# A head's inverse norm brought to all partitions: four transposes on TensorE, or two transfers through DRAM

## The chip, the core and the metric

The kernel runs on one core of a Trainium2 chip. The metric is device time in microseconds (us) of one execution; several executions are run and their median is taken.

The core's engines are called by the profile's names: PE is TensorE (matrix products, and transposes as products with an identity matrix; PEld is its weight load), DVE is VectorE, ACT is ScalarE, POOL is GpSimd, SP is SyncE, which here only issues DMA transfers. POOL issues some transfers too. Each engine works through its own list of instructions in order; when an instruction waits, everything behind it on that engine waits too.

## What is computed

The reference is an encoder trunk of two layers on 512 tokens. The change touches one spot of it, the norm at the end of differential attention. Cut to that:

```python
def diff_attention(qa, ka, va, ..., subln_g, lam_init, cos, sin):
    ...
        s = jnp.einsum('bhcqd,bhckd->bhcqk', qi, k).astype(f32) * scale
        a = jax.nn.softmax(s, axis=-1)
        a = (a[:, :, 0] - lam * a[:, :, 1]).astype(v.dtype)
        return jnp.einsum('bhqk,bhkd->bhqd', a, v)
    ...
    o = rmsnorm(o, subln_g) * (1.0 - lam_init)

def rmsnorm(x, g):
    y = x32 * lax.rsqrt(jnp.mean(x32 * x32, axis=-1, keepdims=True) + EPS)
    return (y * g.astype(jnp.float32)).astype(x.dtype)
```

There are 4 heads and 2 layers, so this norm is computed 8 times. Each time the output `o` of a head has 512 tokens of 128 values; every token has one inverse norm, by which its 128 values are multiplied. The result `ya` goes through `w_br_a`, together with the outputs of a convolution branch and of a neighbourhood attention branch, each under a sigmoid gate. After that come an output projection, a feed-forward block and an embedding gate.

## The kernel before, in words

Activations lie transposed: the 128 partitions hold channels, the free dimension holds the 512 tokens. Nearly all products are made in three parts: a number is split into a high and a low half (`split`, line 162: ACT copies the high half, DVE subtracts to get the low half), and `mm3` (line 175) adds high by high, high by low and low by high. Weights come from DRAM over SP's queue into tile `wr`, are split into `wh` and `wl` by ACT and DVE (`weights`, line 166), and are used by PE; each of these tiles has three buffers. `weights` also keeps the DVE instruction of its low half as `self.low`, and plans the whole load and split some way ahead of its place in the program.

**The order of the work.** PE's instructions run in exactly the order in which the program writes them. For the other engines a planner orders the instructions at build time by priority, which follows the place in the program, and by modelled durations; the chip then runs each engine's list in that fixed order. `behind(i, then)` (line 1064) adds an edge to the planner: instruction `i` comes after `then` on their engine. It adds no wait on the chip.

The program interleaves small jobs with the long projections by a clock of its own. `chunk` (line 115) counts one `mm3` of a 512-column projection; every fourth calls `tick` (line 94). A job is a generator: it emits some instructions, yields a number of ticks, and is continued after so many. `later` (line 107) queues a job with a delay and a gap to the next.

**The layer.** `layer` (line 428) writes: the convolution's gates, neighbourhood attention (four `natten_in`), differential attention (four `diff_in`, one for each head, with other projections between them), the gates for the third branch (`gate_c`), the third branch itself (`branch_c`: eight outputs, one tick each, added into `acc`, tile `gatec_x`), gates of the second branch (`gate_b`), `merge_a` (the first branch's gate and its product with `w_br_a`; the heads' results `ys` are read here), the rest of the convolution, `merge_b`, `w_o`, the feed-forward block and the embedding gate. The 124 taps of the convolution are single DVE instructions (`taps`, line 535), strewn as `background` work over the whole first part of the layer.

**A head.** `diff_in` (line 813) makes queries and keys and queues four `diff_unit` jobs, two ticks apart. Each computes scores for 128 queries (`probs`, line 892: PE scores into one of the two PSUM buffers `sc`, DVE maximum, ACT exponential, DVE combination `diff_a`). Every second job goes on (line 851): after three ticks PE transposes the probabilities, ACT and DVE split them into tile `pt`; after two more ticks PE multiplies with the values into `av`. After the fourth job the head is complete: ACT squares `av` into `sq` (tile tag `ss`, one buffer only) and writes the scaled output `o` (tag `t`). Then `norm` (line 206) runs with the ticks `(1, 2)`:

- after one tick, PE transposes `sq` in four pieces into a PSUM tile (line 213), DVE sums over channels (line 216) and adds the epsilon term (line 221), and POOL raises to the power -0.5 (line 223). The result `col` is a column: partition p, column c holds the inverse norm of token 128c + p.
- after two more ticks, PE transposes each of the four columns of `col`, spread over 128 columns, into a second PSUM tile `bc` (line 227). Every partition then holds the row of all 512 inverse norms.
- `done` (line 884): DVE multiplies `o` by that row (line 885; the profile lists it at line 157, where the helper stands, as diff_t), and ACT and DVE split the product into a tile `y` (five buffers, four of which hold the neighbourhood attention's output until `branch_c` has read it).

The same `norm` serves the main norms and the convolution's norm; these copy the row from PSUM to SBUF (`spread`) and are not changed.

Of the kernel before, what the change touches and what calls it, by code (L numbers as in the profile page):

```python
# [11 lines left out]
F32 = mybir.dt.float32  # L12
# [3 lines left out]
ALU = mybir.AluOpType  # L16
# [4 lines left out]
P = 128  # L21
L = 2
S = 512
# [4 lines left out]
HA = 4  # L28
# [33 lines left out]
class Net:  # L62
# [143 lines left out]
    def norm(self, sq, n, waits, done, spread=True, eps=None):  # L206


        nc = self.nc
        yield waits[0]  # L210
        st = self.ps("tr", (P, 4, P))
        for c in range(4):
            nc.tensor.transpose(st[:, c, :], sq[:, c * P:(c + 1) * P], self.ident)
        with self.tc.high_priority(offset=min(200, self.tc.cur_priority - self.p0) if n == D and self.p0 is not None else 0):
            sm = self.sb("sm", [P, 4])
            nc.vector.tensor_reduce(out=sm, in_=st, op=ALU.add, axis=AX.X)
            ms = self.sb("sm", [P, 4])
            if eps is None:
                nc.vector.tensor_scalar(ms, sm, 1.0 / n, EPS, ALU.mult, ALU.add)
            else:  # L220
                self.stt(ms, sm, 1.0 / n, eps, ALU.mult, ALU.add)
            col = self.sb("rc", [P, 4])
            nc.gpsimd.tensor_tensor(col, ms, self.power, ALU.pow)
        yield waits[1]
        bc = self.ps("tr", (P, 4, P))
        for c in range(4):
            nc.tensor.transpose(bc[:, c, :], col[:, c:c + 1].to_broadcast([P, P]), self.ident)
        bc = bc.rearrange("p a b -> p (a b)")
        done(col, self.spread(bc) if spread else bc)

    def rows(self, col, rb):
        self.col, self.rb = col, rb
# [59 lines left out]
    def build(self):  # L292
        nc, tc, a = self.nc, self.tc, self.a
        self.bufs = dict(wr=3, wh=3, wl=3, h=8, qk=2, kh=2, v=4, pt=2, y=5, z=5, x=4, t=7, rp=4,
                         e=4, a=3, r=2, rb=1, ss=1, sm=8, rc=4, b=2, s=8)
        self.bg, self.w_ahead = BG, 400
        self.pbufs = dict(mm=3, sc=2, tr=2, av=1)
        with tc.tile_pool(name="sb", bufs=1) as self.pool, \
                tc.tile_pool(name="ps", bufs=1, space=PSUM) as self.psum, \
                tc.tile_pool(name="dr", bufs=1, space=DRAM) as dram:  # L300
            xs = dram.tile([KD, P, 512], F32, name="xs")
            self.pis = dram.tile([KD, P, 512], F32, name="pis")
            with tc.manual_schedule(engines={mybir.EngineType.PE}):
                h = self.opening()
                xsrc = a["xT"]
                for i in range(L):
                    h = self.layer(i, h, xsrc, xs)
                    xsrc = xs
# [535 lines left out]
    def diff_unit(self, head, qt, st4, k2, st, box, ys):  # L844

        nc, i = self.nc, self.i
        half, t = qt // 2, qt % 2
        box[qt] = self.probs(st4, k2, qt, box["s0"])
        if t == 0:
            return  # L850
        yield 3
        ats = [box[2 * half], box[2 * half + 1]]
        pps = []
        for kp in range(2):
            pt = self.ps("tr", (P, 2, 256))
            for u in range(2):
                for t in range(2):
                    kc = 2 * kp + u
                    nc.tensor.transpose(pt[:, u, t * P:(t + 1) * P],
                                        ats[t][:, kc * P:(kc + 1) * P], self.ident)  # L860
            pp = self.sb("pt", [P, 2, 2, 256], F32R)
            self.split(pp[:, 0], pp[:, 1], pt)
            pps.append(pp)
        yield 2
        if half == 0:
            box["av"] = self.ps("av")
        av = box["av"]
        cs = slice((head % 2) * P, (head % 2) * P + P)
        for kp in range(2):
            for u in range(2):  # L870
                v = st["v", head // 2][kp][:, u].rearrange("p (a b) -> p a b", a=2)
                self.mm3(av[:, half * 256:half * 256 + 256], v[:, 0, cs], v[:, 1, cs],
                         pps[kp][:, 0, u], pps[kp][:, 1, u], kp * 2 + u == 0, kp * 2 + u == 3)
        if half == 0:
            return

        eps = self.sb("sm", [P, 4])
        self.stt(eps, box["s0"], EPS, box["s0"], ALU.mult, ALU.mult)
        o = self.sb("t", [P, 512])
        sq = self.sb("ss", [P, 512])  # L880
        self.act(sq, av, AF.Square)
        self.act(o, av, AF.Copy, scale=self.subg[:, i:i + 1])

        def done(col, bc):
            self.tt(o, o, bc, ALU.mult)
            y = self.sb("y", [P, 2, 512], F32R)
            self.split(y[:, 0, :], y[:, 1, :], o)
            ys.append(y)

        yield from self.norm(sq, P, (1, 2), done, spread=False, eps=eps)  # L890

    def probs(self, st4, k2, qt, s0):


        nc, i = self.nc, self.i
        qs = slice(qt * P, (qt + 1) * P)
        m = self.sb("s", [P, 10])
        es = []
        for u in range(2):
            sc = self.ps("sc")  # L900
            self.scores(sc, st4, k2, u, qs, slice(0, 512))
            nc.vector.tensor_reduce(out=m[:, u:u + 1], in_=sc, op=ALU.max, axis=AX.X, negate=True)  # L902
            e = self.sb("e" if u else "a", [P, 512])
            self.act(e, sc, AF.Exp, table="exp", bias=m[:, u:u + 1],
                     accum_out=m[:, 3:4] if u else s0[:, qt:qt + 1])
            es.append(e)
        nc.vector.reciprocal(m[:, 4:5], m[:, 3:4])
        self.stt(m[:, 5:6], m[:, 4:5], self.nlam[:, i:i + 1], s0[:, qt:qt + 1],
                 ALU.mult, ALU.mult)
        self.stt(es[0], es[1], m[:, 5:6], es[0], ALU.mult, ALU.add)  # L910
        return es[0]

    def w_o(self, mg, xsrc):
# [553 lines left out]
```

## Time and profile before

| | |
|---|---|
| median of 3 runs | 1777.44 us (1776.35 to 1777.76) |
| span of the profiled execution, first to last instruction | 1776.7 us |
| PE busy in it | 1767.5 us, 99% |
| DVE, ACT, POOL busy | 80%, 50%, 6% |
| granted TensorE clock | 0.999 of full speed |

Of the profiled execution the span is all that is listed; the median of the runs lies 0.7 us above it. The tables below are read as follows. A row of the timeline has the start in us from the span's start, the duration in us, the engine, the line of the program, the operation, what it writes and reads (`diff_t<-diff_t,diff_tr`: phase and tile tag), the shape, and in brackets the idle time of the engine ahead of it with what ended it. Matmuls are pipelined: a matmul's duration in a row is longer than the distance to the next one's start, so the distance of starts tells what PE spends on it. A row of a line's or a tile's view has the number of instructions and the least, median and greatest duration in ns.

### The profile page before, as it was taken

To read this page: it belongs to the slowest core of one execution; us is meant where nothing else is said; L and a number is where in the kernel's file an instruction comes from. 1 tells how busy PE (TensorE), PEld (TensorE's weight loads), DVE (VectorE), ACT (ScalarE), POOL (GpSimd) and SP (SyncE) were. 2 spreads that over 40 slices of the span, in tenths; PEclk is the share of its full clock that TensorE was granted. 3 is DMA by queue.
4 is the path that set the end of the run, shared out by engine and by line. 5 is a ranking of instruction groups with operands and counts; after the bars stand their busy time and mean duration, and the time that the engine had idled before them with its cause. 6 is when DMAs were issued, how large, how long until landed. Compare 5 with 4: busy or idle time off the path is not lost.

```text
span 1776.7 us, 27451 instructions
## 1 busy us (share of the span) xinstructions
PE 1767.5 (99%) x10210; PEld 1559.6 (88%) x10210; DVE 1421.7 (80%) x2418; ACT 894.4 (50%) x1561; POOL 103.0 (6%) x146
## 2 busy tenths in 40 slices
PE   9999999999999999999999999999999999999998
PEld 7888888888899899998888888888888998989987
DVE  7878887998798587787776788889887976867776
ACT  5577555225565254454545765452356643534454
POOL 0000000000111010100000000000001110101000
PEclk9999999999999999999999999999999999999999
DMA  5666641334757366543447655423357664655332
GB/s 202 188 186 176 161 125 42 113 98 140 230 150 193 109 167 160 132 131 123 145 124 198 176 165 149 113 71 95 93 179 198 171 179 115 173 144 151 98 108 92
DMA packets 113509, 256.07 MB, mean 144 GB/s; under 512 B 14560, under 2 KB 19424, under 8 KB 113376
## 3 DMA queue, kind: packets, MB, share of 16 engines
q1 hardware_dynamic: 99984, 229.93, 42.3%
q0 software_dynamic: 12672, 23.07, 8.3%
q8 instruction: 81, 1.33, 0.3%
q10 hardware_dynamic: 720, 1.31, 0.2%
q14 instruction: 52, 0.43, 0.1%
HBM read 215.46 MB, written 7.34 MB: 125 GB/s over the span
## 4 chain that ended last, share of the span: by engine, by line
PE 96%; DVE 2%; ACT 1%; issue 0%; DMA 0%; POOL 0%; ACTq 0%; POOLq 0%; DVEq 0%
PE ffn_mm L1017 4%; PE ffn_mm L1019 4%; PE ffn_mm L177 4%; PE ffn_mm L179 4%; PE ffn_mm L178 4%; PE ffn_mm L1018 4%; PE ffn_sc L1019 3%; PE ffn_sc L1017 3%; PE ffn_sc L1018 3%; PE mergea_mm L177 2%; PE mergea_mm L178 2%; PE mergea_mm L179 2%; PE diff_sc L811 2%; PE gatec_mm L177 2%; PE gatec_mm L178 2%; PE gatec_mm L179 2%
## 5 line engine op out<-in xcount | busy, mean ns | idle before, releaser
L160 DVE SCALAR_TENSOR_TENSOR conv_z<-glu_z,pre_par,conv_z 128x512 f32<-128x512 f32 x240 | 179.4, 748 | 3.3
L143 ACT ACTIVATE ffn_wh<-ffn_wr 128x1024 fp32r<-128x1024 f32 (+1 forms) x92 | 92.7, 1014 | 111.7 <-PE ffn_mm L178 77.1
L987 POOL DMA_DIRECT2D ffn_qk<-w_fu x88 | 78.0, 990 | 605.7 <-DMA ffn_qk<-w_fu 414.7
L157 DVE TENSOR_TENSOR ffn_wl<-ffn_wr,ffn_wh 128x1024 fp32r<-128x1024 f32 (+1 forms) x92 | 107.4, 1173 | 5.4 <-ACT ffn_wh L143 4.9
L157 DVE TENSOR_TENSOR ffn_t<-ffn_mm,wo_rb 128x512 f32<-128x512 f32 (+1 forms) x64 | 38.6, 604 | 67.9 <-PE ffn_mm L179 67.8
L143 ACT ACTIVATE mergea_wh<-mergea_wr 128x1024 fp32r<-128x1024 f32 (+1 forms) x32 | 27.1, 846 | 96.8 <-PE mergea_mm L178 79.6
L143 ACT ACTIVATE ffn_wh<-ffn_qk 128x1024 fp32r<-128x1024 f32 x44 | 46.7, 1060 | 35.9 <-PE ffn_mm L178 15.7
L157 DVE TENSOR_TENSOR ffn_wl<-ffn_qk,ffn_wh 128x1024 fp32r<-128x1024 f32 x44 | 53.8, 1224 | 11.3 <-ACT ffn_wh L143 11.3
L157 DVE TENSOR_TENSOR ffn_t<-ffn_t,ffn_t 128x512 f32<-128x512 f32 (+1 forms) x46 | 31.3, 680 | 31.4 <-ACT ffn_t L143 30.9
L143 ACT ACTIVATE diff_a<-diff_sc,diff_s 128x512 f32<-128x512 f32 x32 | 22.0, 686 | 61.0 <-DVE diff_s L902 61.0
L177 PE MATMUL ffn_mm<-ffn_v,ffn_wh 128*128 128x512 f32 x132 | 51.4, 389 | 0.0
L178 PE MATMUL ffn_mm<-ffn_v,ffn_wh 128*128 128x512 f32 x132 | 51.4, 389 | 0.0
L179 PE MATMUL ffn_mm<-ffn_v,ffn_wl 128*128 128x512 f32 x132 | 51.3, 389 | 0.0
L177 PE MATMUL ffn_mm<-ffn_y,ffn_wh 128*128 128x512 f32 x132 | 51.3, 389 | 0.0
L178 PE MATMUL ffn_mm<-ffn_y,ffn_wh 128*128 128x512 f32 x132 | 51.3, 389 | 0.0
L179 PE MATMUL ffn_mm<-ffn_y,ffn_wl 128*128 128x512 f32 x132 | 51.3, 389 | 0.0
L1019 PE MATMUL ffn_mm<-wo_h,ffn_wl 128*128 128x256 f32 x176 | 49.8, 283 | 0.0
L1019 PE MATMUL ffn_sc<-wo_h,ffn_wl 128*128 128x256 f32 x176 | 49.8, 283 | 0.0
L1018 PE MATMUL ffn_mm<-wo_h,ffn_wh 128*128 128x256 f32 x176 | 49.8, 283 | 0.0
L1018 PE MATMUL ffn_sc<-wo_h,ffn_wh 128*128 128x256 f32 x176 | 49.8, 283 | 0.0
L1017 PE MATMUL ffn_sc<-wo_h,ffn_wh 128*128 128x256 f32 x176 | 49.8, 283 | 0.0
L1017 PE MATMUL ffn_mm<-wo_h,ffn_wh 128*128 128x256 f32 x176 | 49.8, 283 | 0.0
(876 smaller groups left out, 6588.6 us busy)
## 6 DMA issues: line engine op xcount, KB each, us to landing
ffn_qk<-w_fu POOLq DMA_DIRECT2D x88, 256.0 KB, 5.7
ffn_wr<-w_fg SPq DMA_DIRECT2D x44, 512.0 KB, 3.7
ffn_wr<-w_fd SPq DMA_DIRECT2D x32, 448.0 KB, 3.9
ffn_r<-w_fu SPq DMA_DIRECT2D x44, 256.0 KB, 3.7
ffn_qk<-w_fg SPq DMA_DIRECT2D x44, 256.0 KB, 4.3
ffn_qk<-w_fu SPq DMA_DIRECT2D x44, 256.0 KB, 4.6
natten_wr<-w_in SPq DMA_DIRECT2D x16, 512.0 KB, 4.3
natten_b<-bias SPq DMA_DIRECT2D x32, 256.0 KB, 4.0
```

Source lines behind the costliest of these rows:

```text
L143: i = self.nc.scalar.activation(out, in_, func, **kw)
L157: return self.nc.vector.tensor_tensor(out, a, b, op)
L160: return self.nc.vector.scalar_tensor_tensor(out, a, s, b, op0, op1)
L177: mm(out, wh, ah, start=first, stop=False)
L178: mm(out, wh, al, start=False, stop=False)
L179: mm(out, wl, ah, start=False, stop=last)
L811: self.nc.tensor.matmul(out, st4[:, u, qs], st[:, ks], start=n == 0, stop=n == 1)
L987: nc.gpsimd.dma_start(q, wu[:, lo], accum_op=ALU.add)
L1017: mm(out, wh[:, c], bh, start=first and k == 0, stop=False, skip_group_check=True)
L1018: mm(out, wh[:, c], bl, start=False, stop=False, skip_group_check=True)
L1019: mm(out, wl[:, c], bh, start=False, stop=k == 3, skip_group_check=True)
```

## The change

For the heads' norms (`spread=False`) the four transposes of `col` are gone. Instead POOL issues two transfers: `col` is written to a row of 512 numbers in DRAM (one row for each head and layer), element by element, since the column order has to be turned into token order; then that row is read into all 128 partitions of `sq`, which is free by then. The job then yields the remaining ticks at once, and the ticks are now `(1, 4)`: `done` is written four ticks after the sum of squares, not two. In `done` the multiplication reads the row from `sq` in SBUF instead of from PSUM, and it gets two edges: behind the low half of the latest weights (`self.low`), and behind the latest instruction of the heads' probabilities (`self.prob`, which `diff_unit` and `probs` now keep).

```diff
+        if not spread:
+            rows, self.rowed = self.nrm[self.rowed], self.rowed + 1
+            with nc.allow_non_contiguous_dma(reason="column to row"):
+                nc.gpsimd.dma_start(rows.rearrange("(c p) -> p c", p=P), col)
+            nc.gpsimd.dma_start(sq, rows[None, :].to_broadcast([P, S]))
+            yield sum(waits[1:])
+            return done(col, sq)
         yield waits[1]
         bc = self.ps("tr", (P, 4, P))
         for c in range(4):
             nc.tensor.transpose(bc[:, c, :], col[:, c:c + 1].to_broadcast([P, P]), self.ident)
         bc = bc.rearrange("p a b -> p (a b)")
-        done(col, self.spread(bc) if spread else bc)
+        done(col, self.spread(bc))
...
+            self.nrm, self.rowed = dram.tile([L * HA, S], F32, name="nrm"), 0
...
-            self.split(pp[:, 0], pp[:, 1], pt)
+            self.prob = self.split(pp[:, 0], pp[:, 1], pt)
...
         def done(col, bc):
-            self.tt(o, o, bc, ALU.mult)
+            i = self.tt(o, o, bc, ALU.mult)
+            self.behind(i, self.low)
+            self.behind(i, self.prob)
...
-        yield from self.norm(sq, P, (1, 2), done, spread=False, eps=eps)
+        yield from self.norm(sq, P, (1, 4), done, spread=False, eps=eps)
...
-        self.stt(es[0], es[1], m[:, 5:6], es[0], ALU.mult, ALU.add)
+        self.prob = self.stt(es[0], es[1], m[:, 5:6], es[0], ALU.mult, ALU.add)
```

## The prediction

> **What bounds the kernel now.** First the page: busy shares and the chain of work that ended last.
>
> ```profile
> span 1776.7 us, 27451 instructions
> ...
> PE 1767.5 (99%) x10210; PEld 1559.6 (88%) x10210; DVE 1421.7 (80%) x2418; ACT 894.4 (50%) x1561; POOL 103.0 (6%) x146
> ...
> PE 96%; DVE 2%; ACT 1%; issue 0%; DMA 0%; POOL 0%; ACTq 0%; POOLq 0%; DVEq 0%
> ```
>
> PE is the bound: busy 99% of the span, 96% of the chain. So PE work that disappears is worth its full time, and the other engines cost nothing until they make PE wait. All that follows asks two things: how much PE work goes, and whether anything new comes late for PE.
>
> **What goes.** The view of line 227 counts the removed transposes, and the timeline around the first group (head 0 of the first layer) and the last (head 3 of the second) shows what they take.
>
> ```profile
> L227 PE MATMUL diff_tr<-pre_ident,diff_rc x32: 270/272/273, 224.9 to 1194.4; 128*128 128x128 f32 x32
> ```
>
> ```profile
> 224.65 0.39 PE L179 MATMUL diff_mm<-glu_h,diff_wl 128*128 128x512 f32 x1
> ...
> 224.88 0.60 PE L227 MATMUL diff_tr<-pre_ident,diff_rc 128*128 128x128 f32 x4
> ...
> 225.23 0.47 PE L811 MATMUL diff_sc<-diff_qk 128*128 128x512 f32 x1
> ...
> 225.51 0.69 DVE L157 TENSOR_TENSOR diff_t<-diff_t,diff_tr 128x512 f32<-128x512 f32 x1 [0.74 <-PE diff_tr L227]
> 225.54 0.40 PE L811 MATMUL diff_sc<-diff_x,diff_qk 128*128 128x512 f32 x1
> ...
> 225.78 0.40 PE L811 MATMUL diff_sc<-diff_qk 128*128 128x512 f32 x1
> ```
>
> ```profile
> 1194.07 0.60 PE L227 MATMUL diff_tr<-pre_ident,diff_rc 128*128 128x128 f32 x4
> ...
> 1194.42 0.48 PE L177 MATMUL branchc_mm<-natten_y,branchc_wh 128*128 128x512 f32 x1
> ...
> 1194.74 0.39 PE L178 MATMUL branchc_mm<-natten_y,branchc_wh 128*128 128x512 f32 x1
> ...
> 1194.97 0.39 PE L179 MATMUL branchc_mm<-natten_y,branchc_wl 128*128 128x512 f32 x1
> ```
>
> Durations overlap, so I take distances of starts. A 512-column matmul takes 0.23 us to the next start (224.65 to 224.88, 1194.74 to 1194.97). In the first group, from the start of the transposes to the second matmul behind them is 225.54 - 224.88 = 0.66 us; without them one matmul of 0.23 us would fill that stretch. The group therefore costs 0.43 us: 0.35 for the four transposes, and some 0.08 because the first matmul behind them takes longer. The last group gives 1194.74 - 1194.07 - 0.23 = 0.44 us. The 32 transposes make 8 groups: 8 x 0.435 = **3.5 us** off PE, 0.2% of the span. That PE comes straight back with the next matmul in both groups says that nothing else holds it there.
>
> On DVE the multiplication itself stays, only its second operand moves from PSUM to SBUF.
>
> ```profile
> L157 DVE TENSOR_TENSOR diff_t<-diff_t,diff_tr x8: 679/687/689, 225.5 to 1195.5; 128x512 f32<-128x512 f32 x8
> ```
>
> ```profile
> L157 DVE TENSOR_TENSOR ffn_t<-ffn_t,ffn_t 128x512 f32<-128x512 f32 (+1 forms) x46 | 31.3, 680 | 31.4 <-ACT ffn_t L143 30.9
> ```
>
> From PSUM 687 ns, from SBUF alone 680 ns: nothing. The wait of 0.74 us for the transposes goes; what DVE waits for next is the transfer.
>
> **What is added: a chain of two transfers.** After POOL's power come an issue, a landing in DRAM, a wait of POOL for it, a second issue and a landing in `sq`.
>
> ```profile
> L223 POOL TENSOR_TENSOR diff_rc<-diff_sm,pre_power x8: 1006/1008/1504, 219.2 to 1191.3; 128x4 f32<-128x4 f32 x8
> ```
>
> ```profile
> 219.16 1.02 POOL L223 TENSOR_TENSOR diff_rc<-diff_sm,pre_power 128x4 f32<-128x4 f32 x1 [55.51 <-DVE diff_sm L160]
> ...
> 311.75 1.50 POOL L223 TENSOR_TENSOR diff_rc<-diff_sm,pre_power 128x4 f32<-128x4 f32 x1 [29.29 <-DVE diff_sm L160]
> 415.26 1.01 POOL L223 TENSOR_TENSOR conv_rc<-conv_sm,pre_power 128x4 f32<-128x4 f32 x1 [102.01 <-PE pin_sc L178]
> ```
>
> ```profile
> L987 POOL DMA_DIRECT2D ffn_qk<-w_fu x88: 862/886/1245, 453.6 to 1643.7; - x88
> ...
> DMA to landing us min/median/max: 3.8/5.7/10.0
> ```
>
> ```profile
> branchc_wr<-w_br_c SPq DMA_DIRECT2D x16, 256.0 KB, 2.7
> ...
> pis<-pin_t SPq DMA_DIRECT2D x12, 256.0 KB, 2.1
> ```
>
> No row shows a transfer of 4-byte pieces, nor one row read 128 times. The nearest are POOL's own 256 KB transfers: 5.7 us from issue to landing, 10.0 at most. From below, SP's store to DRAM lands in 2.1 us and its 256 KB load in 2.7. So the chain takes between 2.1 + 2.7 = 4.8 and 2 x 10.0 = 20 us. I take 2 x 5.7 = **11.4 us**, since the same queue issues them: the second has the same size, the first has fewer bytes but many more pieces. It ends 11.4 us after the power: 220.2 + 11.4 = 231.6 for the first head, 313.25 + 11.4 = 324.7 for head 3.
>
> Behind the waiting POOL nothing stands: its next work after head 0 is the next head's power 31 us later, after head 3 the convolution's at 415.26. SP's queue isn't passed. The 256 KB per head go beside weights that SP loads well ahead of PE; eight heads add 2 MB to 256 MB moved.
>
> **Where the multiplication now stands.** Its order on DVE matters, since DVE stops there until the row has landed.
>
> *Heads 0 to 2.* By its edge the multiplication comes behind the combination that ends the unit started with the old transposes, and by its place in the program (two ticks later) ahead of the next unit's maximum.
>
> ```profile
> 228.77 0.75 DVE L160 SCALAR_TENSOR_TENSOR diff_a<-diff_e,diff_s,diff_a 128x512 f32<-128x512 f32 x1
> ...
> 233.81 0.69 DVE L902 TENSOR_REDUCE diff_s<-diff_sc 128x1 f32<-128x512 f32 x1
> ...
> 236.75 0.16 DVE L907 RECIPROCAL diff_s<-diff_s 128x1 f32<-128x1 f32 x1 [0.78 <-ACT diff_e L143]
> ```
>
> ```profile
> 240.40 0.39 PE L811 MATMUL diff_sc<-diff_qk 128*128 128x512 f32 x1
> ```
>
> So it stands between 229.5 and 233.8, and the row lands at 231.6: a stop of DVE of 0 to 2 us. What is queued behind is the maximum at 233.81; PE needs the score buffers again at 240.40, and ACT has read them by 236.75. That is 3.6 us of room; only a row that lands after about 237.4, a chain of 17 us, would reach PE.
>
> *Head 3.* Here no more units follow, and `branch_c` runs at one tick per output, so two ticks are 24 matmuls, 24 x 0.23 = 5.5 us.
>
> ```profile
> 314.10 0.68 DVE L157 TENSOR_TENSOR conv_ss<-conv_z,conv_z 128x512 f32<-128x512 f32 x1
> ...
> 315.96 0.68 DVE L157 TENSOR_TENSOR diff_t<-diff_t,diff_tr 128x512 f32<-128x512 f32 x1
> ...
> 320.98 0.68 DVE L157 TENSOR_TENSOR gatec_x<-gatec_x,branchc_mm 128x512 f32<-128x512 f32 x1
> 321.57 1.22 DVE L157 TENSOR_TENSOR gateb_wl<-gateb_wr,gateb_wh 128x1024 fp32r<-128x1024 f32 x1
> 322.71 1.89 DVE L157 TENSOR_TENSOR diff_y<-diff_t,diff_y 128x512 fp32r<-128x512 f32 x3
> ...
> 357.49 0.68 DVE L157 TENSOR_TENSOR conv_ss<-conv_ss,conv_z 128x512 f32<-128x512 f32 x1
> ```
>
> ```profile
> 329.04 0.39 PE L179 MATMUL gateb_mm<-glu_h,gateb_wl 128*128 128x512 f32 x1
> ...
> 339.47 0.39 PE L177 MATMUL mergea_mm<-diff_y,mergea_wh 128*128 128x512 f32 x1
> ```
>
> Before, the multiplication stood ahead of the product with `branch_c`'s fifth output; two outputs later is ahead of the one at 320.98. If DVE stops there until 324.7, that is 3.7 us. First for PE behind it are the low halves of a gate's weights, ready at 322.79, used at 329.04: 6.25 us of room. The heads' own results are ready at 324.6 and not read until 339.47, so their lateness costs nothing; `sq` and `o` are held longer, but `o` waited for a `y` buffer anyway (the splits of three heads run together at 322.71), and the convolution's sum at 314.10, which needs the same single buffer, may slide, as it is not added to before 357.49. The cover holds with 2.5 us to spare; if it is gone, each further us costs 1 us of PE in each layer.
>
> **A rule against the change.** The rows first: POOL's power took 1.50 us at 311.75 where the median is 1.01, and in that stretch DVE has hardly a gap.
>
> ```profile
> 310.00:330.00 20.00, 20.00 (x92) 16.54 (x91) 19.88 (x31) 7.24 (x10) 1.50 (x1) 1.00 0.45 132
> ```
>
> DVE is the fourth entry, 19.88 of 20 us. As a mechanism of this kernel: if POOL could not issue while DVE works, the first transfer would go out only when DVE itself stops at the multiplication, 320.98, and land 11.4 us later at 332.4. The stop of 11.4 us, less 6.25 of room, costs 5.2 us in each layer: 1773.9 + 10.4 = 1784.3. Against it speak the 88 issues beside a DVE busy most of the time: 862 to 1245 ns, no outlier. The Trainium skill, page "SBUF — State Buffer", section "SBUF: two separate sides", states such a lock: transfers issued from GpSimd can't have their descriptors written while VectorE runs a two-port instruction, and one went from about 620 to 3100 ns. By that figure, as an estimate, the two issues would lengthen the chain by 5 us to 16.4 and cost about 2.4 us a layer; the trace bears out only some tenths of a us.
>
> **The rivals.**
>
> 1. *The row comes late* (slower). Same place, head 3: PE loses what the chain exceeds 13.9 us by (7.7 to DVE's stop, 6.25 of room), twice. From 15.7 us the gain is gone, from 17.5 the kernel is slower by over 0.2%, and from 17 heads 0 to 2 pay too. At the upper bound of 20 us head 3 costs 6 us a layer, and six heads some 2.6 us each: 1773.9 + 12 + 16 = 1802. For it: the 10.0 us landings, and pieces of 4 bytes that no row shows. Against: the median of 5.7. With the lock above, 1784 to 1802 in all.
> 2. *Part is given back*: a chain of 14 to 17 us, or DVE's shifted order making PE wait here and there: 1775 to 1778.
> 3. *More than the transposes*: with a PSUM buffer less in use and DVE's order shifted, a short wait elsewhere goes, 1 to 1.5 us: 1772.6.
> 4. *The change does not free PE*: another supplier paces it at once, 1777.4. Against it: PE returns without a gap behind each group.
>
> **How the numbers follow.** The span is 1776.7 and the median 1777.44, 0.7 us above it; I set the saving against the median: 1777.44 - 3.5 = **1773.9**. Chances: forecast 0.62 (own range 1773.2 to 1774.9), late row or lock 0.12, part given back 0.15, more 0.06, PE not freed 0.05. The range 1772.9 to 1778.0 holds the forecast, the partial loss and no change, 0.82; it leaves out the late row and most of the larger gain. A measurement of this kernel can tell some 0.2% from no change, which is 3.55 us; the forecast's 3.5 lies on that line, so I split its 0.62 in halves. Faster: 0.31 + 0.06 = 0.37; same: 0.31 + 0.15 + 0.05 = 0.51; slower: 0.12.
>
> **What would show it.** Right: line 227 has no rows of diff_tr, PE's matmuls follow each other at 0.23 us where the groups stood, the two landings after each power end within 14 us, DVE's idle time ahead of diff_t is under 4 us, and no matmul of gateb or diff waits behind it. Wrong: PE gaps right after diff_t's idle time (rival 1), first issues of several us (the lock), or PE gaps elsewhere (rival 2).

## The result, and the profile after

| | before | changed |
|---|---|---|
| median of 4 runs each, us | 1776.89 (1775.95 to 1777.76) | 1820.13 (1818.99 to 1821.21) |
| ratio, 95% interval | | 1.0243 [1.0229, 1.0256] |
| profiled execution, span, us | 1776.7 | 1817.7 |

The change makes the kernel 43 us slower, 2.4%. The forecast was 1773.9 and the range ended at 1778.0.

The head of the page and of its chain of waits:

```profile
span 1817.7 us, 27415 instructions
...
PE 1773.6 (98%) x10178; PEld 1558.8 (86%) x10178; DVE 1420.0 (78%) x2418; ACT 892.7 (49%) x1561; POOL 113.9 (6%) x162
...
PE 31%; issue 2%; DMA 1%; DVE 0%; POOL 0%; ACT 0%; POOLq 0%; ACTq 0%; DVEq 0%
```

PE has 32 instructions fewer (10210 to 10178), so the transposes did go, and yet PE is busy 6 us longer: below we see matmuls that last up to twice as long after a gap. The chain adds up to only a third of the span, since following it back breaks off on the way; it can't be read as a share here, and the waits of PE take its place (waited for, total us, times, longest):

```profile
PE gateb_mm L177 <- ACT diff_y L143: 21.6, 2, 11.1
PE diff_sc L819 <- ACT diff_a L143: 10.3, 4, 4.1
PE diff_tr L213 <- ACT diff_ss L143: 3.5, 4, 0.9
```

These 35 us are new. Two of the waits, one in each layer, make 21.6 of them: behind head 3, where the third branch ends. The rest stands in heads 0 to 2. In the page's list of groups, the multiplication shows the idle time ahead of it on DVE:

```profile
L157 DVE TENSOR_TENSOR diff_t<-diff_t,diff_ss 128x512 f32<-128x512 f32 x8 | 5.5, 693 | 62.8 <-DMA diff_ss<-nrm 62.8
```

Its own cost is as forecast (693 ns, before 687), but DVE stands still in front of it for 62.8 us, 4.4 to 11.6 us each time and 7.9 on average, and the releaser is the second transfer. The view of the column tile gives the first transfer, the view of the row's tile the second (least, median, greatest from issue to landing):

```profile
L227 POOL DMA_DIRECT2D nrm<-diff_rc x8: 806/815/963, 219.5 to 1226.4; - x8
...
DMA to landing us min/median/max: 9.8/10.0/10.9
```

```profile
L228 POOL DMA_DIRECT2D diff_ss<-nrm x8: 551/553/582, 229.9 to 1238.0; - x8
...
DMA to landing us min/median/max: 3.4/4.0/6.2
```

The write of 2 KB takes longer (10.0 us) than the read of 256 KB (4.0 us).

**Head 0, layer 0.** POOL's timeline, then DVE's:

```profile
218.14 1.02 POOL L223 TENSOR_TENSOR diff_rc<-diff_sm,pre_power 128x4 f32<-128x4 f32 x1 [55.48 <-DVE diff_sm L160]
219.49 0.96 POOL L227 DMA_DIRECT2D nrm<-diff_rc  x1 [0.33 <-POOL diff_rc L223]
229.88 0.58 POOL L228 DMA_DIRECT2D diff_ss<-nrm  x1 [9.43 <-DMA nrm<-diff_rc]
```

```profile
227.16 0.75 DVE L160 SCALAR_TENSOR_TENSOR diff_a<-diff_e,diff_s,diff_a 128x512 f32<-128x512 f32 x1
236.14 0.69 DVE L157 TENSOR_TENSOR diff_t<-diff_t,diff_ss 128x512 f32<-128x512 f32 x1 [8.22 <-DMA diff_ss<-nrm]
236.75 1.22 DVE L157 TENSOR_TENSOR gatec_wl<-gatec_wr,gatec_wh 128x1024 fp32r<-128x1024 f32 x1
...
240.95 1.28 DVE L912 TENSOR_REDUCE diff_s<-diff_sc 128x1 f32<-128x512 f32 x2
```

```profile
242.50 0.52 PE L819 MATMUL diff_sc<-diff_qk 128*128 128x512 f32 x1 [3.44 <-ACT diff_a L143]
```

From the end of the power (219.16) to the start of the multiplication the chain takes 17.0 us; over all eight heads it takes 14.6 to 17.6. DVE stops at 227.9; when it goes on, six other pieces of work stand ahead of the next maximum, which comes at 240.95 instead of 233.81, and PE waits 3.44 us for its scores buffer.

**Head 3, layer 0.** POOL's power ends at 323.74 (322.22 + 1.52), the row has landed by 339.39, a chain of 15.6 us. DVE, then PE:

```profile
325.21 0.68 DVE L157 TENSOR_TENSOR gatec_x<-gatec_x,branchc_mm 128x512 f32<-128x512 f32 x1
...
326.41 1.54 DVE L160 SCALAR_TENSOR_TENSOR conv_z<-glu_z,pre_par,conv_z 128x512 f32<-128x512 f32 x2
339.39 0.69 DVE L157 TENSOR_TENSOR diff_t<-diff_t,diff_ss 128x512 f32<-128x512 f32 x1 [11.44 <-DMA diff_ss<-nrm]
340.00 0.68 DVE L157 TENSOR_TENSOR gatec_x<-gatec_x,branchc_mm 128x512 f32<-128x512 f32 x1
340.60 1.22 DVE L157 TENSOR_TENSOR gateb_wl<-gateb_wr,gateb_wh 128x1024 fp32r<-128x1024 f32 x1
```

```profile
329.91 0.39 PE L179 MATMUL branchc_mm<-natten_y,branchc_wl 128*128 128x512 f32 x1
340.83 0.77 PE L177 MATMUL gateb_mm<-glu_h,gateb_wh 128*128 128x512 f32 x1 [10.53 <-ACT diff_y L143]
341.39 0.63 PE L178 MATMUL gateb_mm<-glu_h,gateb_wh 128*128 128x512 f32 x1
```

Of a stop of 11.44 us PE loses 10.53: nearly no room. The bracket names ACT's copy of the same product, but that is not what this matmul reads. By the program there are three PSUM buffers for these accumulators (`mm=3`); the third branch's last three outputs fill them, and the gate's first matmul needs the one that the product at 340.00 reads. That product stands directly behind the multiplication, ends at 340.68, and PE starts at 340.83; in experiment 8 the profile names this product itself for the same wait. Then the matmuls last 0.77 and 0.63 us instead of 0.39 for a while. The view by windows shows why: its third number from the end is the granted clock, half of full speed from 340.8 to 345.4 us and full speed behind that.

```profile
340.80:345.40 4.60, 4.57 (x11) 3.31 (x12) 4.60 (x7) 0.96 (x2) 0.00 (x0) 0.52 0.23 65
345.40:350.00 4.60, 4.60 (x22) 3.78 (x21) 4.60 (x8) 1.12 (x2) 0.00 (x0) 1.00 0.49 166
```

Over the whole run the granted clock is 0.992, before 0.999.

### The profile page after: what moved, and what is told of

Its sections match the earlier page's. It is cut to its first block, busy times and chain, and to the rows that moved or that the text cites. A ratio compares the mean times of both kernels' runs of the same rounds, so it can differ in the third digit from the quotient of the medians.

```text
span 1817.7 us, 27415 instructions
## 1 busy us (share of the span) xinstructions
PE 1773.6 (98%) x10178; PEld 1558.8 (86%) x10178; DVE 1420.0 (78%) x2418; ACT 892.7 (49%) x1561; POOL 113.9 (6%) x162
## 5 line engine op out<-in xcount | busy, mean ns | idle before, releaser
L157 DVE TENSOR_TENSOR diff_t<-diff_t,diff_ss 128x512 f32<-128x512 f32 x8 | 5.5, 693 | 62.8 <-DMA diff_ss<-nrm 62.8
L1028 PE MATMUL ffn_mm<-wo_h,ffn_wh 128*128 128x256 f32 x176 | 49.8, 283 | 0.0
```

The lines of the kernel that those rows point to most:

```text
L157: return self.nc.vector.tensor_tensor(out, a, b, op)
L1028: mm(out, wh[:, c], bl, start=False, stop=False, skip_group_check=True)
```

## The experiments

Theory A: all of the loss is DVE's stop in order at the multiplication, and what stands behind it. Theory B: the transfers themselves disturb other work, whoever waits for them. They were compared with runs of the kernel before on the same chip (1776.7 to 1776.96); ratios are to those, with 95% intervals.

**1. The multiplication later.** The chain gets its time, all else stays.

```diff
-        yield from self.norm(sq, P, (1, 4), done, spread=False, eps=eps)
+        yield from self.norm(sq, P, (1, 10 if head == HA - 1 else 6), done, spread=False, eps=eps)
```

> The changed kernel with done placed later: (1, 6) ticks for heads 0 to 2, (1, 10) for head 3, nothing else. Theory A (DVE stands in order at the multiplication until a chain of two transfers of 16 to 17 us has ended, and PE starves behind it): by the edges the multiplication now comes some 8 us later in the first three heads and behind the low halves of the last gate and of merge_a's first weights in the last, DVE waits under 5 us there and PE does not wait at all; the 3.5 us of the transposes are then gained, 1773.5 (1772.9 to 1775). Rival B (the transfers or their POOL issues disturb PE, DVE or the weights' transfers by themselves): still 1785 or more. Rival C (the two edges shift DVE's other work badly): no better than 1800.

1788.47 us, 1.0067 [1.0054, 1.0079]. DVE's idle time ahead of all eight multiplications is gone, and 31.7 us of the 43 with it. So most of the loss is the stop; but the kernel is still 11.5 us slower than before, which the stop can't explain, and A alone falls.

**2. The transfers beside the old transposes, unread.** The kernel before, with both transfers added; a quarter of the row (64 KB in all partitions together) goes into a spare tile, and nothing waits for it.

```diff
+        if not spread:
+            rows, self.rowed = self.nrm[self.rowed], self.rowed + 1
+            with nc.allow_non_contiguous_dma(reason="column to row"):
+                nc.gpsimd.dma_start(rows.rearrange("(c p) -> p c", p=P), col)
+            nc.gpsimd.dma_start(self.sb("gap", [P, GAP], bufs=1)[:, :P], rows[None, :P].to_broadcast([P, P]))
         yield waits[1]
...
```

> The kernel before, with the two transfers issued beside its transposes; nobody reads what they bring, and the second fills only 128 of the 512 columns (64 KB) of a spare tile. Theory A: no more than noise, 1776.5 to 1777.8, although the column write takes 10 us again. Rival B: a good part of the 43 us, 1785 or more.

1788.75 us, 1.0067 [1.0054, 1.0081]: 11.8 us, as much as experiment 1 had left, with no reader at all. B is right about this part.

**3. The new ticks and edges alone.** Transposes as before, but with the new ticks and the two edges; no transfers. The edit is against the changed kernel.

```diff
         if not spread:
-            rows, self.rowed = self.nrm[self.rowed], self.rowed + 1
-            with nc.allow_non_contiguous_dma(reason="column to row"):
-                nc.gpsimd.dma_start(rows.rearrange("(c p) -> p c", p=P), col)
-            nc.gpsimd.dma_start(sq, rows[None, :].to_broadcast([P, S]))
             yield sum(waits[1:])
-            return done(col, sq)
-        yield waits[1]
+        else:
+            yield waits[1]
...
-        done(col, self.spread(bc))
+        done(col, self.spread(bc) if spread else bc)
```

> The other half of the change alone: four transposes as before, no transfers, but (1, 4) ticks and both edges on the multiplication. Theory A: the row is there half a us after it is asked for, DVE does not stop, 1776 to 1778. Rival C: slower than 1785.

1776.97 us, 1.0000 [0.9990, 1.0009]. Ticks and edges cost nothing by themselves. But the run doesn't price the place that the multiplication has in the changed kernel, since here the planner puts it later: in head 0 behind three products of the rotation, and in head 3 behind two low halves of the gate's weights instead of ahead of both.

```profile
233.46 0.69 DVE L157 TENSOR_TENSOR diff_t<-diff_t,diff_tr 128x512 f32<-128x512 f32 x1
```

```profile
321.56 1.22 DVE L157 TENSOR_TENSOR gateb_wl<-gateb_wr,gateb_wh 128x1024 fp32r<-128x1024 f32 x1
...
323.90 0.68 DVE L157 TENSOR_TENSOR diff_t<-diff_t,diff_tr 128x512 f32<-128x512 f32 x1
```

What the changed kernel's own place costs when the row comes early is seen in the next experiment.

**4. Pieces of 16 bytes.** The changed kernel, with the column written so that each partition's four numbers lie side by side: 128 pieces instead of 512. The row is then in another order, so each token is multiplied by another token's norm.

```diff
-                nc.gpsimd.dma_start(rows.rearrange("(c p) -> p c", p=P), col)
+                nc.gpsimd.dma_start(rows.rearrange("(p c) -> p c", p=P), col)
```

> The changed kernel with the column written as 128 pieces of 16 bytes in place of 512 of 4 bytes: the row then holds the inverse norms in another order, so that each token is multiplied by another token's. Same places on DVE, same bytes. Theory A with the 512 pieces as the price of the first transfer: it lands in 3 to 5 us in place of 10, DVE's stops shrink by 5 to 7 us each, head 3 costs PE 4 to 6 us a layer and the others next to nothing: 1782 to 1790. Rival D (a fixed cost of a small write from POOL to DRAM): it still takes 9 us or more and the time stays at 1816 to 1821.

1777.74 us, 1.0008 [0.9999, 1.0017]. The same 2 KB over the same queue; the column's tile shows

```profile
DMA to landing us min/median/max: 1.7/1.8/4.6
```

instead of 10.0, and sooner than the 3 to 5 us expected, so the time lies below the expected 1782 to 1790. One letter order in the address takes back 42 us: the multiplications stand where they stood in the changed kernel, and only three still stop DVE, 10.7 us in all, for which PE pays 2.7 us at the gate.

**5. The column alone.** Experiment 2 without the second transfer.

> e2_beside without the second transfer: transposes as before, only the column written in 512 pieces of 4 bytes, that nobody reads. Theory A1: all of e2_beside's loss, 1786 to 1790. Rival E: back at 1777 or a part of the way.

1788.27 us, 1.0063 [1.0049, 1.0077]. The 4-byte write does it; the broadcast read adds nothing that can be told.

What it disturbs is in the view of the tile of the rope rotation, by which SP shifts the queries and keys in blocks of 32 partitions. Before, then with the column beside it:

```profile
DMA to landing us min/median/max: 1.9/2.7/5.4
```

```profile
  DMA diff_rp<-diff_rp: 11.8, 2
...
DMA to landing us min/median/max: 1.9/2.8/11.8
```

Four rotations are issued 3.5 to some 5 us behind the column, and DVE, which had never waited for one, waits 5.9 us in each layer. PE then waits for the next squares and scores, 7.5 us in all, and is busy 4.4 us longer than before (1771.9 us). The DMA view of the window 215 to 245 us, in 40 slices of 0.75 us, shows the stand-still itself; before, and then experiment 5:

```profile
GB/s 216 194 205 210 186 224 169 350 137 0 0 0 44 104 355 399 153 5 11 0 0 0 87 93 262 380 139 76 205 191 213 101 0 82 137 437 82 259 309 93
```

```profile
GB/s 186 208 221 191 208 183 289 268 12 1 0 0 44 0 0 11 93 22 33 22 22 27 22 38 330 320 292 265 361 120 11 0 0 0 0 205 219 197 167 0
...
diff_rp<-diff_rp SPq DMA_DIRECT2D x8, 64.0 KB, 9.1
...
nrm<-diff_rc POOLq DMA_DIRECT2D x1, 2.0 KB, 10.1
```

Before, the rotations go through at 104 to 399 GB/s from 224.8 us on (14th to 17th slice). With the column under way the engines move 0 to 93 GB/s until 233 us, some 3 us past its landing (issued at 220.1, landed 10.1 later), and then 330. The zeros ahead of 224 us stand in both rows and are not the column's doing.

**6. Both transfers unread, 16-byte pieces.** Experiment 2 with the edit of experiment 4.

> e2_beside (transposes as before, two transfers beside them that nobody reads, the second of 64 KB) with the column written in 128 pieces of 16 bytes. Theory A1: the 12 us go, 1776.5 to 1778. Rival E: unchanged at 1787 to 1790.

1777.39 us, 1.0002 [0.9993, 1.0011]; the column lands in 1.9 us (1.7 to 3.6). What the transfers cost others is the pieces' doing.

**7. Pieces of 8 bytes.** Experiment 5 with 256 pieces.

```diff
+                nc.gpsimd.dma_start(rows.rearrange("(c p e) -> p c e", p=P, e=2),
+                                    col.rearrange("p (c e) -> p c e", e=2))
```

> The kernel before with the column write alone, unread, beside the transposes, as 256 pieces of 8 bytes (the earlier run wrote 512 of 4, and took 1788.27). It asks for the size of the piece. If each piece costs the same, 256 land in about 5 us, the rope transfers beside it are late by some 2 to 4 us and the time is 1777 to 1781. If the 4 bytes themselves are the slow form, it lands in 2 to 3 us as the 16-byte pieces did, and the time is 1777. If anything below 16 bytes is slow, 8 to 10 us and 1783 to 1788.

1777.45 us, 1.0002 [0.9993, 1.0011]. The column's tile, at half the pieces:

```profile
DMA to landing us min/median/max: 3.5/5.2/6.0
```

So it is the number of pieces, not a slow form at 4 bytes: 512 take 10.6 us (median of experiment 5), 256 take 5.2, about 20 ns for each piece; 128 take 1.8 to 2.0, some 15 ns each. Number and size of the pieces always changed together, since the 2 KB stay. PE loses nothing. In head 0 this column has landed (220.8 + 4.0 us) by about the time the rotations are issued, from 224.3 us on, and the greatest landing of the rotation's tile is 6.2 us; the run therefore doesn't show what 256 pieces would do to transfers that run beside them for long.

**8. The column issued by SP.** To see if it is GpSimd's queue that is slow.

```diff
-                nc.gpsimd.dma_start(rows.rearrange("(c p) -> p c", p=P), col)
+                nc.sync.dma_start(rows.rearrange("(c p) -> p c", p=P), col)
```

> The changed kernel with the column's 512 pieces issued on SP's queue in place of POOL's. Theory A1: the pieces take 8 us or more on that queue too, the time stays within 1810 to 1825. Rival F (POOL's queue is what makes the write slow): it lands in 2 to 3 us, 1790 or less.

1824.32 us, 1.0267 [1.0253, 1.0281]. The column lands in 11.4 us (9.7 to 12.1): another queue doesn't help. For PE's wait at the gate the profile here names the product into `acc`, not ACT's copy:

```profile
PE gateb_mm L177 <- DVE gatec_x L157: 24.5, 2, 12.6
```

**9. Without the two edges.** The changed kernel, but the planner alone places the multiplication.

```diff
-            self.behind(i, self.low)
-            self.behind(i, self.prob)
```

> The changed kernel without the two edges, so that the planner alone places the multiplication. Theory (DVE stops in order until the row lands, and the loss is the length of the stop less the room of what is queued behind): the multiplication of some heads then stands earlier than now, the stops grow by what it moves, and the time is 1825 to 1845. Rival (the edges themselves are what forces DVE's order, and the stop is theirs): without them it is put later by the planner, after ready work, and the time falls to about 1790, which the short-lived wait on the transfer and the rope rotations leave.

1855.82 us, 1.0445 [1.0429, 1.0461]. The direction is the theory's, the size is more than it gave. The planner puts the multiplication ahead of the maxima of a unit that is already waiting:

```profile
222.95 1.28 DVE L157 TENSOR_TENSOR diff_pt<-diff_tr,diff_pt 128x512 fp32r<-128x512 f32 x2
236.39 0.69 DVE L157 TENSOR_TENSOR diff_t<-diff_t,diff_ss 128x512 f32<-128x512 f32 x1 [12.16 <-DMA diff_ss<-nrm]
237.00 1.28 DVE L910 TENSOR_REDUCE diff_s<-diff_sc 128x1 f32<-128x512 f32 x2
```

The stop grows from 8.22 to 12.16 us here and to 93.0 in all; the edges do help, they are only not enough.

**10. Late places and 16-byte pieces: what the transposes are worth.** Experiment 1 with the edit of experiment 4.

> The kernel of the first experiment (the multiplication of heads 0 to 2 two ticks later, of head 3 six ticks later) with the column written as 128 pieces of 16 bytes, without a change of the queries: the row then lies in another order, so each token is multiplied by another token's inverse norm. With late places and short transfers neither the stop of DVE nor the stand-still of other transfers is left, and no matmul is added; only the removed transposes remain. If their 3.5 us is PE time that comes back, 1773.4 (1772.5 to 1774.5). If another supplier paces PE at once and the transposes were free, 1776.9. DVE's idle time ahead of the multiplication: none by either.

1775.00 us, 0.9989 [0.9980, 0.9998], over 11 runs against 21, above the expected 1772.5 to 1774.5. The profile:

```profile
span 1773.2 us, 27413 instructions
...
PE 1764.5 (100%) x10178; PEld 1556.6 (88%) x10178; DVE 1420.6 (80%) x2418; ACT 893.8 (50%) x1561; POOL 113.0 (6%) x162
```

The medians differ by 1.9 us, with an interval of 0.4 to 3.6 us. The gain exists; the whole 3.5 us lies at the interval's edge. The profiled spans, 1773.2 and 1776.7, would give 3.5, but 1776.7 is the longest span that the 21 runs before show (1774.3 to 1776.7); by the medians of all spans, 1773.1 and 1775.0, the gain is 1.9 again. PE's busy time falls by 3.0 us (1767.5 to 1764.5), and a wait of 0.8 us for a score buffer is new.

**11. and 12. Versions that keep the computation.** Short pieces need the tokens in the order 4p + c. Experiment 11 lets the scores read every fourth query and ACT put the output back into order; experiment 12 puts the queries into that order once a head, where ACT and DVE split them.

```diff
...
-        qs = slice(qt * P, (qt + 1) * P)
+        qs = slice(qt, S, 4)
...
```

> e1_late with the column written in 128 pieces of 16 bytes, and right: each of a head's four units takes every fourth query, so that a column's four numbers are neighbours in the row, and ACT puts the output o back into token order as it copies it. Theory A1 (the 512 pieces of 4 bytes hold up all other transfers for about 8 us, some 12 us of PE in all, and the stop of DVE costs the rest): both are gone, the transposes' 3.5 us stay gained, 1773.5 (1772.9 to 1775). Rival E (the 256 KB read of the row, or the POOL issues, are what disturbs): 1785 or more. The strided queries could cost PE or ACT some tenths of a us each, 1774 to 1776.

```diff
...
+                low, by4 = rot.bitcast(F32R), raw.rearrange("d (p c) -> d c p", c=4)
+                self.split(nat.rearrange("d (c p) -> d c p", c=4),
+                           low.rearrange("d (c p) -> d c p", c=4), by4)
...
```

> A version that keeps the whole computation: late places, 16-byte pieces, and the tokens of the queries put into the order 4p + c once a head, where ACT and DVE split the rotated queries (16 instructions in all read by strides), so that the scores read their columns side by side again; ACT puts the output back into token order. If the strided columns of the scores were what the earlier valid version gave its gain back to, 1773.5 to 1775.0. If the strided reads of ACT and DVE ahead of the first scores make PE wait, 1776 to 1778.

1776.99 us, 0.9999 [0.9990, 1.0008], and 1775.84 us, 0.9996 [0.9987, 1.0006]; both lie above the 1773.5 to 1775.0 hoped for. With the strided columns of experiment 11 the scores' matmuls last 401 and 394 ns (medians of the two forms) where experiment 10 has 389, and PE is busy 2.0 us longer than there (1766.5). Experiment 12 is without that (1764.4), but neither version can be told from the kernel before by its runs. The column's detour can be made harmless; it can hardly be made to pay.

**The sum.** Before 1776.93; without transposes, with nothing in the way 1775.00 (experiment 10): -1.9. With 4-byte pieces 1788.47 (experiment 1): +13.5, other transfers' delay. With the multiplication in the change's place 1820.13: +31.7, DVE's stop, which grew to its length by the same pieces. Experiment 4 shows that shared root: with 16-byte pieces both parts go.

## Why the prediction was wrong, point by point

Three steps failed: the price of the column's write, the room behind the multiplication, and the effect of the write on other transfers, which was put at nothing. What the transposes are worth was right in mechanism.

- *PE is the bound, and 8 groups cost 3.5 us.* Right in mechanism; in size the runs show 1.9 us (0.4 to 3.6), and PE's busy time 3.0.
- *The chain, 2 x 5.7 = 11.4 us.* This term failed, in its first half. The prediction let "fewer bytes but many more pieces" cancel out; the pieces decide, for the same bytes in 128 pieces took 1.8 us. The column took 10.0 us, the row 4.0 (up to 6.2), the chain 14.6 to 17.6, well inside its bounds of 4.8 and 20. The value was chosen by the queue that the nearest row shared, and experiment 8 shows that the queue hardly matters.
- *Heads 0 to 2: room until a landing at 237.4.* The landing came at 236.1 and PE waited all the same. The step "what is queued behind is the maximum" left out what lies between. The timeline before has five instructions there, which the prediction's rows pass over:

```profile
230.05 1.23 DVE L157 TENSOR_TENSOR gatec_wl<-gatec_wr,gatec_wh 128x1024 fp32r<-128x1024 f32 x1 [0.53 <-ACT gatec_wh L143]
231.19 0.68 DVE L157 TENSOR_TENSOR diff_rp<-diff_rp,diff_r 128x512 f32<-128x512 f32 x1
231.79 0.74 DVE L160 SCALAR_TENSOR_TENSOR conv_z<-glu_z,pre_par,conv_z 128x512 f32<-128x512 f32 x1
232.45 0.69 DVE L157 TENSOR_TENSOR diff_rp<-diff_rp,diff_r 128x512 f32<-128x512 f32 x1
233.17 0.69 DVE L157 TENSOR_TENSOR diff_rp<-diff_rp,diff_rp 128x512 f32<-128x512 f32 x1
```

  With the multiplication and the output's own low half they take 4.8 us (236.14 to 240.95), which DVE now does behind the landing. The maximum came 7.1 us late, 8.5 against PE, which was 1.3 us ahead by then (242.50 - 3.44 = 239.06 instead of 240.40). PE waited 3.44, so there was even more room than the 3.6 us forecast, 5.0, and it was used up.
- *Head 3: a stop of 3.7 us and 6.25 us of room.* This failed twice. The planner puts the multiplication one product earlier than taken, and also ahead of the low half that the gate needs first (340.60). And the room was looked for at the gate's weights, where the first need was the accumulator's buffer: three buffers, all full, the first of them freed by the product directly behind the multiplication. The room was 11.44 - 10.53 = 0.9 us.
- *"The 256 KB per head go beside weights that SP loads well ahead."* True of the second transfer, but the step asked only what the bytes do, and of SP's queue only whether it is passed. The rotations, which are not loaded ahead, were not looked at, and no rival had them. Experiments 2 and 5 show the price, 11.3 to 11.8 us, and experiment 6 shows that it goes with the short write.
- *Rivals.* The late row was the right mechanism, at 0.12. Its price was too low: at its own terms a chain of 15.6 us costs (15.6 - 13.9) x 2 = 3.4 us at head 3, where PE waited 21.6. It inherited the room of 6.25 us from the forecast, and so did the lock's 1784.3.
- *The lock.* Not seen: the issues took 0.81 to 0.96 us and 0.55 to 0.58, and the delay comes after them, with the write issued by SP as well.

## What to carry to other kernels

Price a transfer by its pieces before its bytes, and ask which other transfers are under way at that moment, not only whose queue it is on. When an instruction will wait on an in-order engine, list everything between it and the first instruction that the bound engine needs, and count buffers being freed as needs, not only data. An operation taken off the bound engine is worth at most its own time, so a replacement with a latency must be placed by the worst landing, or it is better left alone.

## What the runs showed of the hardware

- A write to DRAM of 2 KB in 512 pieces took 10.0 to 10.6 us, in 256 pieces 5.2, in 128 pieces 1.8 to 2.0 (medians), from GpSimd's queue; from SP's, 512 took 11.4.
- While the 512 were under way in experiment 5, the rotations on another queue landed in 11.1 to 11.8 us instead of 4.0 to 4.5, and all DMA engines together moved 0 to 93 GB/s. In the changed kernel a 512 KB load of weights beside head 3's column landed in 11.6 us; before, such loads landed there in 3.4 (median).
- Why they stood still is open. The Trainium skill, page "DMA: Bandwidth & Descriptors", section "Queues, rings and completion order", says that a DMA engine drains a whole packet of one queue, several pieces long, before it turns to another. In the windows of experiments 5, 7 and 10 that hold one column and no row, the queue shows 32 packets each time, for 512, 256 and 128 pieces alike, by division 16, 8 and 4 pieces to a packet; here the row of experiment 5.

```profile
q0 software_dynamic: 32, 0.00, 0.6%
```

  A packet that holds more pieces could block an engine longer. But the last number is the share of the 16 engines' time in this window of 30 us: the 32 packets took 2.9 us of engine time together, some 0.2 us an engine, by these records. That is far less than the stand-still, which also lasted 3 us past the landing, so the packets' order alone doesn't explain it here, and no run tried it by itself.
- Why a piece costs 20 ns is open too. The same page of the Trainium skill says in its section "Specifications" that pieces under 512 bytes are done by reading and writing back, but no run here separates that.
- After a wait PE's granted clock falls to about half. In the changed kernel it was 0.52 for 4.6 us behind a gap of 10.5 us, and 0.55 from 242.5 to 246.0 us behind the gap of 3.44 us. In experiment 5 a gap of 2.28 us, ended at 252.2, was followed by 0.98 until 254.0 and then 0.50 until 257.2. So a wait of PE costs more than its length.
